# Seven-product quads in two value chunks and in one more run of both down projections

## The chip, the cores and the metric

The kernel runs on one NeuronCore of a Trainium2 chip. The metric is the device time of one execution in microseconds; before the change it is 2053.36 us, the median of three runs (2053.22 to 2055.54). Engines are named as the profile names them: PE is TensorE (PEld its weight loads), DVE is VectorE, ACT is ScalarE, POOL is GpSimd, SP is SyncE, which here only issues DMAs.

## The reference

Two decoder layers over 256 tokens of width 2048, in float32. Each layer is attention, a residual with LayerNorm, a gated feed-forward, and a residual with LayerNorm:

```python
q, k, v = split(x @ w_qkv)                   # layer 1: 16 heads of 128, causal, T5 bias
attn = softmax(q k^T * scale + bias) v @ w_o
h = layer_norm(ALPHA * h + attn)
hc = causal_conv3(h @ w_up) + conv_b         # 2 x 5504 features
g, u = split(hc)
h = layer_norm(ALPHA * h + (gelu(g) * u) @ w_down)
```

With 256 tokens and blocks of 256, layer 1's block-sparse attention is plain causal attention. Layer 2 takes a window of 128 tokens with learned sinks, and its 16 query heads share 4 key and value heads. The result must match in float32.

## The kernel before

**Precision.** TensorE multiplies in a rounded format, so every operand is kept as a high part and a low part: for weights ScalarE copies the raw tile to `wh` (L160) and VectorE subtracts to get `wl` (L169). A product takes three matmuls: high x high, high x low, low x high (L530 to L532; L385 to L387 in the value projections). The fourth is dropped.

**Halves.** Weights stream from HBM as *halves*, 128 x 1024 floats (512 KB), two blocks of 128 x 512. SP loads each into one of six `raw` tiles (L141); the split goes into one of four pairs `wh`, `wl`; TensorE takes them in order. The next load of a raw tile is issued once VectorE's split has read it. One half is one *slot* of the written schedule: `at(n, f)` puts f into the agenda n slots ahead, and `take` (L204) first asks for the splits up to three halves ahead and then runs the agenda. So each engine's order is fixed by the program, and an operation of the agenda stands between the splits on VectorE's queue.

**Two kinds of products.** Queries, keys and up projections hold the weights still (`ws_unit`, two halves, 32 matmuls). Values, output and down projections hold the tokens still and move the weights: a *plain* half has 2 blocks x 2 token tiles x 3 = 12 matmuls of 512 columns.

**Quads.** Where the plan of a projection says so (`PLAN_O`, `PLAN_DOWN`, made by `_mixed`), a 2 x 2 group of tokens and output chunks is done with seven products in place of eight (Strassen-Winograd). One *run* of quads covers four blocks of the contraction and a pair of 512-wide output chunks: seven halves of 6 matmuls (`SEVEN`) in place of four plain halves of 12. It needs

- combined weights, T1 to T4: *presums* (L426) load a quad's four blocks (two DMAs of 512 KB on SP), combine them with four VectorE operations (L436) and store them to HBM (two DMAs on POOL); they run during earlier projections, one quad every 6 or 8 slots, through one buffer `gb`;
- combined activations: `sums` (L582), three steps in successive slots: `whole` (L588), `combine` (three or four operations, L599) and `split` (ScalarE L604, VectorE L605). They are kept in `xT` and a further tile;
- the accumulators P1, P5, P6, P7 (PSUM banks named `at`), which `fold` adds into the result at the end of a chunk pair. The plain products and the rest go to four banks named `acc`, one for each (chunk, token tile).

`PLAINS` and `PLAINS_O` say how many plain halves stand before, between and after the runs. In a down projection (43 blocks, four chunks) each chunk pair has six runs; in the first pair 2 plain halves stand between most runs, in the second pair 1, and 15 at the end. The last eight halves of a projection are its *window*: first all of token tile 0, then all of token tile 1, so that LayerNorm of tile 0 runs under the matmuls of tile 1. An accumulator is emptied (`evac`: L547 or L549 adds it into the residual, L553 takes the LayerNorm statistics) after both token tiles of its chunk are complete; for odd chunks one and two slots later.

**Layer 1's attention** goes over four groups of four heads: a value chunk of 8 plain halves (`v_group`), then for each head a query unit and a key unit, with the softmax of the head before it spread over the next slots. Each bias table for the softmax is spread through HBM: a row table `ud`, four DMAs to `band` (L297; layer 1's on POOL, layer 2's on ACT), and four loads of `bias` (L301). The residual input comes in two DMAs of 1 MB on SP at slots 55 and 70.

Of the kernel before, what the change touches and what calls it, by code (L numbers as in the profile page):

```python
# [2 lines left out]

# [8 lines left out]
F32 = mybir.dt.float32  # L12
# [35 lines left out]
PLAINS = ((5, 2, 2, 2, 2, 0, 6), (0, 1, 1, 1, 1, 0, 15))  # L48
NQ_O = 4
PLAINS_O = (5, 3, 0)  # L50
SEVEN = (("B11", "B21"), ("T1", "T3"), ("T2", "T4"), ("B22", "B22"), ("B11", "B21"), ("T1", "T3"), ("T2", "T4"))
# [10 lines left out]
def _mixed(c, groups, plain, p0):  # L62

    plan, at = [], 0
    for i, g in enumerate(groups):
        plan += plain[at:at + g]
        at += g
        if i < len(groups) - 1:
            plan += [tuple((b, p0 + 2 * i + p, c) for b, p in zip(bs, ps)) for bs, ps in zip(SEVEN, PAIR_OF)]
    assert at == len(plain)  # L70
    return plan
# [3 lines left out]
PLAN_DOWN = [h for c in range(2) for h in _mixed(c, PLAINS[c], _plain(range(2 * NQ, FT), (2 * c, 2 * c + 1)), 0)]  # L75
QUADS = {}
for _l in range(2):
    QUADS[2 * _l] = [(2 * _l, 0, NH // 2 - NQ_O + p) for p in range(NQ_O)]
    QUADS[2 * _l + 1] = [(2 * _l + 1, c, p) for c in range(2) for p in range(NQ)]
ORDER = [q for li in range(4) for q in QUADS[li]]  # L80
AHEAD_OF = {0: QUADS[0] + QUADS[1][:8], 1: QUADS[1][8:] + QUADS[2], 2: QUADS[3][:4], 3: QUADS[3][4:]}
# [7 lines left out]
def _stages():  # L89

    for l in range(2):
        yield [None] * (48 if l else 96), 0
# [6 lines left out]
def trunk(ctx: ExitStack, tc: tile.TileContext, wst, wsum, xT_in, x_in, relb, onehot, umask, sinks, conv_in, ln_g, ln_b, out):  # L99
# [128 lines left out]

    def load_input(pool, tables):
# [65 lines left out]
    def spread_bias(l, h0, h1):  # L295
        a = ud[l, h0:h1, :]
        (nc.scalar if l else nc.gpsimd).dma_start(band[l, h0:h1], bass.AP(tensor=a.tensor, offset=a.offset + P - 1,  # L297
# [128 lines left out]
    def presums(quads, first_slot, pitch):  # L426
# [18 lines left out]
        for i, q in enumerate(quads):  # L445
            m = first_slot + pitch * i
            at(m, load, q, 0)
            at(m + 1, load, q, 1)
            for j, x in enumerate(steps):
                at(m + 4 + j, step_of, *x)  # L450
                if j % 2:
                    at(m + 4 + j, store, q, j // 2)

    def project_out(src, plan, li, homes, preload, turnover=None, quad_blocks=None):
# [41 lines left out]
        banks, used, owed = {}, {}, {}  # L496

        def token(x, t):
            return x[:, t * P:(t + 1) * P], x[:, T + t * P:T + (t + 1) * P]

        def keys(e):
            b, k, n = e
            if b == "plain":
                return [(n, t) for t in range(2)]
            n0, n1 = 2 * n, 2 * n + 1
            return [{"B11": ("P1", n), "B21": (n0, 0), "T1": ("P5", n), "T3": ("P7", n), "T2": ("P6", n), "T4": (n0, 1),
                     "B22": (n1, 0)}[b]]

        def target(e):
            b, k, n = e  # L510
            if b == "plain":
# [578 lines left out]
```

## Time and profile before

| | |
|---|---|
| runs, median (lowest to highest) | 2053.36 us (2053.22 to 2055.54) |
| the profiled execution, its own time | 2053.82 us |
| its span, first to last instruction | 2052.1 us |
| mean granted TensorE clock | 0.998 |
| mean DMA rate | 276 GB/s |
| first value chunk of the third group | 154.5 to 176.3 us |
| output projection, layer 1 | 298 to 388 us |
| up projection, layer 1 | 388 to 870 us |
| down projection, layer 1 | 870 to 1090 us |
| down projection, layer 2 | 1821 to 2040 us |

Of the profile, a group's row has its line, engine, operation, tiles, count, busy time, mean duration and idle time before it; a row of waits has what waited, for what, us in total, times, longest; a row of the order in time has start, duration, engine, line, operation, and in brackets the idle time before it with what ended it. A stretch has for each engine its busy time and instruction count, then the granted clock, the DMA engines' busy share and GB/s.

### The profile page before, as it was taken

To read this page: it belongs to the slowest core of one execution; us is meant where nothing else is said; L and a number is where in the kernel's file an instruction comes from. 1 tells how busy PE (TensorE), PEld (TensorE's weight loads), DVE (VectorE), ACT (ScalarE), POOL (GpSimd) and SP (SyncE) were. 2 spreads that over 40 slices of the span, in tenths; PEclk is the share of its full clock that TensorE was granted. 3 is DMA by queue.
4 is the path that set the end of the run, shared out by engine and by line. 5 is a ranking of instruction groups with operands and counts; after the bars stand their busy time and mean duration, and the time that the engine had idled before them with its cause. 6 is when DMAs were issued, how large, how long until landed. Compare 5 with 4: busy or idle time off the path is not lost.

```text
span 2052.1 us, 29718 instructions
## 1 busy us (share of the span) xinstructions
PE 2036.1 (99%) x10908; PEld 1759.3 (86%) x10908; DVE 1675.9 (82%) x2399; ACT 1138.3 (55%) x1676; POOL 75.4 (4%) x138
## 2 busy tenths in 40 slices
PE   9999999999999999999999999999999999999997
PEld 7888888988888888888888888898888888888886
DVE  5676678888888888899896788978888888889887
ACT  5444456455555555566673556545555555556672
POOL 0100000000000000000000000000000000000000
PEclk9999999999999999999999999999999999999999
DMA  8888988468888888888994767838888888889893
GB/s 297 287 281 328 320 287 313 162 238 282 289 288 273 282 296 269 285 286 329 323 366 156 261 217 252 285 126 275 281 286 283 279 283 291 272 266 328 312 361 150
DMA packets 158722, 566.64 MB, mean 276 GB/s; under 512 B 19008, under 2 KB 21376, under 8 KB 157296
## 3 DMA queue, kind: packets, MB, share of 16 engines
q1 hardware_dynamic: 136064, 492.74, 70.7%
q0 software_dynamic: 20160, 69.64, 8.7%
q10 hardware_dynamic: 2352, 2.36, 0.3%
q8 instruction: 86, 1.41, 0.3%
q14 instruction: 60, 0.49, 0.1%
HBM read 503.78 MB, written 65.06 MB: 277 GB/s over the span
## 4 chain that ended last, share of the span: by engine, by line
PE 98%; DVE 1%; DMA 0%; ACT 0%; issue 0%; ACTq 0%; DVEq 0%
PE acc L322 39%; PE acc L324 20%; PE acc L530 7%; PE acc L531 7%; PE acc L532 7%; PE at L532 2%; PE at L531 2%; PE at L530 2%; PE acc L386 2%; PE acc L385 2%; PE acc L387 2%; PE acc L349 1%; PE acc L361 1%; PE at L722 1%; PE at L755 1%; PE at L748 1%
## 5 line engine op out<-in xcount | busy, mean ns | idle before, releaser
L169 DVE TENSOR_TENSOR wl<-raw,wh 128x1024 fp32r<-128x1024 f32 (+1 forms) x754 | 898.8, 1220 | 186.4 <-ACT wh L160 163.9
L160 ACT ACTIVATE wh<-raw 128x1024 fp32r<-128x1024 f32 (+1 forms) x754 | 770.4, 1052 | 207.9 <-PE acc L532 104.5
L322 PE MATMUL acc<-xT,wh 128*128 128x512 f32 x3456 | 832.8, 392 | 0.0
L322 PEld LDWEIGHTS acc<-xT,wh 128*128 128x128 f32 x3456 | 641.1, 188 | 128.6
L324 PEld LDWEIGHTS acc<-xT,wl 128*128 128x128 f32 x3456 | 444.2, 190 | 12.4
L324 PE MATMUL acc<-xT,wl 128*128 128x256 f32 x3456 | 452.5, 284 | 0.0
L909 ACT ACTIVATE h<-acc 128x256 f32<-128x256 f32 x172 | 66.4, 386 | 409.1 <-PE acc L324 203.1
L917 DVE SCALAR_TENSOR_TENSOR c<-h,cw,c 128x255 f32<-128x255 f32 x344 | 165.4, 481 | 9.1 <-ACT c L913 2.8
L436 DVE TENSOR_TENSOR gb<-gb 128x512 f32<-128x512 f32 x224 | 153.5, 685 | 5.9 <-DMA gb<-in_wsum_dram 5.9
L910 DVE TENSOR_TENSOR h<-acc,h 128x256 f32<-128x256 f32 x172 | 72.7, 423 | 64.2 <-ACT h L909 64.2
L440 POOL DMA_DIRECT2D ws<-gb x112 | 59.8, 534 | 1412.1 <-DVE gb L436 1360.3
L530 PE MATMUL acc<-wh,up 128*128 128x512 f32 x275 | 107.0, 389 | 0.0
L531 PE MATMUL acc<-wl,up 128*128 128x512 f32 x275 | 107.0, 389 | 0.0
L532 PE MATMUL acc<-wh,up 128*128 128x512 f32 x275 | 107.0, 389 | 0.0
L913 ACT ACTIVATE c<-h,cw 128x256 f32<-128x256 f32 x172 | 101.7, 591 | 0.0
L530 PE MATMUL acc<-wh,st 128*128 128x512 f32 x174 | 68.8, 395 | 0.0
L531 PE MATMUL acc<-wl,st 128*128 128x512 f32 x174 | 67.8, 390 | 0.0
L532 PE MATMUL acc<-wh,st 128*128 128x512 f32 x174 | 67.8, 390 | 0.0
L831 ACT ACTIVATE qT<-acc 128x256 f32<-128x256 f32 x32 | 12.3, 385 | 91.3 <-PE acc L324 65.9
L532 PEld LDWEIGHTS acc<-wh,up 128*128 128x128 f32 x275 | 51.6, 188 | 10.7
L530 PEld LDWEIGHTS acc<-wh,up 128*128 128x128 f32 x275 | 51.6, 188 | 10.7
L531 PEld LDWEIGHTS acc<-wl,up 128*128 128x128 f32 x275 | 51.6, 188 | 10.6
(193 smaller groups left out, 2152.5 us busy)
## 6 DMA issues: line engine op xcount, KB each, us to landing
raw<-in_wst_dram SPq DMA_DIRECT2D x694, 512.0 KB, 5.2
gb<-in_wsum_dram SPq DMA_DIRECT2D x112, 512.0 KB, 7.6
ws<-gb POOLq DMA_DIRECT2D x112, 512.0 KB, 6.2
raw<-ws SPq DMA_DIRECT2D x112, 512.0 KB, 5.6
bias<-band POOLq DMA_DIRECT2D x8, 512.0 KB, 7.2
band<-ud POOLq DMA_DIRECT2D x4, 512.0 KB, 12.7
band<-ud ACTq DMA_DIRECT2D x4, 512.0 KB
res<-in_x_dram SPq DMA_DIRECT2D x2, 1024.0 KB, 9.4
```

Of the source, the lines that this page charges most:

```text
L160: nc.scalar.activation(wh[:, c], raws[s][:, c], AF.Copy)
L169: nc.vector.tensor_tensor(out=wl[:, c], in0=raws[s][:, c], in1=wh[:, c].bitcast(F32), op=ALU.subtract)
L322: nc.tensor.matmul(acc, w, xT[:, k, :], start=(k == 0), stop=(k == ends[0]))
L324: nc.tensor.matmul(acc[:, 0:T], w, xT[:, k, 0:T], start=False, stop=(k == ends[1]))
L436: nc.vector.tensor_tensor(out=w[:, o:o + 512], in0=a, in1=b, op=op)
L530: nc.tensor.matmul(acc, sh, wh, start=first, stop=False)
L531: nc.tensor.matmul(acc, sh, wl, start=False, stop=False)
L532: nc.tensor.matmul(acc, sl, wh, start=False, stop=last)
L909: nc.scalar.activation(h, acc[:, T:2 * T], AF.Copy)
L910: nc.vector.tensor_tensor(out=h, in0=acc[:, 0:T], in1=h, op=ALU.add)
L913: nc.scalar.activation(c, h, AF.Identity, bias=w[:, 3:4], scale=w[:, 2:3])
L917: nc.vector.scalar_tensor_tensor(c[:, d:T], h[:, 0:T - d], w[:, 2 - d:3 - d], c[:, d:T], op0=ALU.mult, op1=ALU.add)
```

## The change

In layer 1 the value chunks of the third and fourth group are computed together by `v_pair`, before the third group's heads: `PLAN_V` has 5 plain halves, a run, 3 plain halves, a run (22 halves in place of 16). Their accumulators are copied by ScalarE and added by VectorE into the value tiles.

In both down projections the second chunk pair gets a seventh run. All seven now follow each other without a plain half between them, in the order 4, 0, 1, 2, 3, 5, 6, and the 15 remaining plain halves follow. The sums of the seventh run have all four parts; they are computed eleven slots into the second pair and written over the sums of run 4 (`last_sums`), which is why run 4 goes first.

An accumulator is emptied as soon as it alone is complete, also inside the window (`late`): chunk 2 now ends in the window's first half. The code of quads is moved into a function `mixed` that both users call, without another change.

The presums have eight more quads (64 in place of 56). In layer 1's attention they start at slot 16 in place of 22, in the up projections they are spread evenly over 152 slots (one in about 7) in place of one in 8. Layer 1's bias spreading goes to slots 4, 6, 8, 10 (three of the four on ACT's queue), layer 2's from slots 40, 47, 76, 82 to 76, 82, 88, 94.

```diff
-PLAINS = ((5, 2, 2, 2, 2, 0, 6), (0, 1, 1, 1, 1, 0, 15))
+MORE = 2
+RUNS = (range(6), (4, 0, 1, 2, 3, 5, 6))
+PLAINS = ((5, 2, 2, 2, 2, 0, 6), (0, 0, 0, 0, 0, 0, 0, 15))
...
+PLAN_V = _mixed(1, PLAINS_O, _plain(range(KB - 2 * NQ_O), (2, 3)), KB // 2 - NQ_O)
-PLAN_DOWN = [h for c in range(2) for h in _mixed(c, PLAINS[c], _plain(range(2 * NQ, FT), (2 * c, 2 * c + 1)), 0)]
+PLAN_DOWN = [h for c in range(2) for h in _mixed(c, PLAINS[c], _plain(range(2 * (NQ + MORE * c), FT), (2 * c, 2 * c + 1)), 0, RUNS[c])]
...
-AHEAD_OF = {0: QUADS[0] + QUADS[1][:8], 1: QUADS[1][8:] + QUADS[2], 2: QUADS[3][:4], 3: QUADS[3][4:]}
+QUADS[4] = [(4, 1, KB // 2 - NQ_O + p) for p in range(NQ_O)]
+ORDER = [q for li in (4, 0, 1, 2, 3) for q in QUADS[li]]
+AHEAD_OF = {0: QUADS[4] + QUADS[0] + QUADS[1][:6], 1: QUADS[1][6:] + QUADS[2], 2: QUADS[3][:4], 3: QUADS[3][4:]}
...
+    def last_sums():
+        flat = xT[:, KB - 4:KB, :].rearrange("p a b -> p (a b)")
+        return flat.rearrange("p (h q s c) -> p h q s c", h=2, q=2, s=4)
...
-        (nc.scalar if l else nc.gpsimd).dma_start(band[l, h0:h1], bass.AP(tensor=a.tensor, offset=a.offset + P - 1,
+        (nc.scalar if l or h0 else nc.gpsimd).dma_start(band[l, h0:h1], bass.AP(tensor=a.tensor, offset=a.offset + P - 1,
...
         def late(t, i):
             last = i == WINDOW - 1
+            for n in range(NCH - 1):
+                if (n, t) not in evacuated and done((n, t)):
+                    evacuated.add((n, t))
+                    evac(n, t)
...
+            if ns == 3:
+                for j, f in enumerate(sums(NQ // 2)):
+                    at(whole + 11 + j, f)
...
             for n in range(NCH):
-                if n not in evacuated and done((n, 0), (n, 1)):
-                    evacuated.add(n)
-                    for t in range(2):
-                        at((t + 1) * (n % 2), evac, n, t)
+                for t in range(2):
+                    if (n, t) not in evacuated and done((n, t)):
+                        evacuated.add((n, t))
+                        at(t * (n % 2) * (ns == 3), evac, n, t)
...
-                at(4 + 5 * i, spread_bias, 0, h, h + 4)
-                at((40, 47, 76, 82)[i], spread_bias, 1, h, h + 4)
-            at((4 + 5 * i, 4 * i)[l], load_bias, bias, l, h, h + 4)
+                at(4 + 2 * i, spread_bias, 0, h, h + 4)
+                at((76, 82, 88, 94)[i], spread_bias, 1, h, h + 4)
+            at((5 + 2 * i, 4 * i)[l], load_bias, bias, l, h, h + 4)
...
+        def v_pair():
+            src = lambda k: xT[:, k, :]
+            k0 = KB - 2 * NQ_O
+            vts, begun = {}, set()
...
+            def into(t, n, a):
+                if n not in vts:
+                    vts[n] = pool.tile([P, 2, 512], F32, name="vt", bufs=2)
+                d = vts[n][:, t, :]
+                if (t, n) in begun:
+                    nc.vector.tensor_tensor(out=d, in0=d, in1=a, op=ALU.add)
+                else:
+                    begun.add((t, n))
+                    nc.scalar.activation(d, a, AF.Copy)
+
+            parted = mixed(src, PLAN_V, k0 // 2, lambda i: 4, lambda i: xT[:, k0 + 4 * i:k0 + 4 * i + 4, :], place, into)
+            mv = Moving(src, 0)
+            for i in range(len(PLAINS_O) - 1):
+                for j, f in enumerate(parted.sums(i)):
+                    at(sum(PLAINS_O[:i]) + 7 * i + j, f)
+            evacuated = set()
+            for half in PLAN_V:
+                blocks = [mv.block() for _ in range(2)]
+                for e, w in zip(half, blocks):
+                    for tgt in parted.target(e):
+                        parted.product(*tgt, *w)
+                step()
...
+            parted.fold(1)
...
-        presums(AHEAD_OF[2 * l], 3 if l else 22, 8 if l else 6)
+            presums(ahead, [16 + 6 * i for i in range(len(ahead))])
...
-            presums(AHEAD_OF[2 * l + 1], 4, 8)
+            presums(ahead, [4 + 152 * i // (len(ahead) - 1) for i in range(len(ahead))])
```

More of the change, by code (lines that the diff above doesn't have):

```diff
@@ L2 @@
 from contextlib import ExitStack
+from types import SimpleNamespace
 import numpy as np
@@ L59, in _plain, with _mixed @@
     return [tuple(blocks[i:i + 2]) for i in range(0, len(blocks), 2)]
-def _mixed(c, groups, plain, p0):
+def _mixed(c, groups, plain, p0, runs=None):
     plan, at = [], 0
@@ L68, in _mixed @@
         if i < len(groups) - 1:
-            plan += [tuple((b, p0 + 2 * i + p, c) for b, p in zip(bs, ps)) for bs, ps in zip(SEVEN, PAIR_OF)]
+            r = runs[i] if runs else i
+            plan += [tuple((b, p0 + 2 * r + p, c) for b, p in zip(bs, ps)) for bs, ps in zip(SEVEN, PAIR_OF)]
     assert at == len(plain)
@@ L424, in acc_tile, with presums @@
         return psum.tile([P, 512], F32, name="acc")
-    def presums(quads, first_slot, pitch):
+    def presums(quads, slots):
         area = gbp.tile([P, 2, D], F32, name="gb")
@@ L444, in presums @@
                  (1536, b21, w[:, 1024:1536], ALU.subtract))
-        for i, q in enumerate(quads):
-            m = first_slot + pitch * i
+        for m, q in zip(slots, quads, strict=False):
             at(m, load, q, 0)
@@ L494, in project_out @@
         ag, rs = {}, {}
[L496 to L511, printed above, removed]
[L512 to L535 removed]
         def zs(t, n):
             return res[:, t, n * 512:(n + 1) * 512]
+        parted = mixed(src, plan, p0, lambda i: ns + (2 * i >= NQ), quad_blocks, lambda i: xsum(i, ns) if 2 * i < NQ else last_sums(), lambda t, n, a: into(t, n, a))
+        banks, target, product, done, fold, sums = (parted.banks, parted.target, parted.product, parted.done, parted.fold,
+                                                    parted.sums)
         paired = {e[2] for half in plan for e in half if e[0] == "B11"}
@@ L823, in v_group, with place @@
             return vt
+        def v_pair():
+            src = lambda k: xT[:, k, :]
+            k0 = KB - 2 * NQ_O
+            vts, begun = {}, set()
+            def place(i):
+                flat = st[:, NH // 2 + 4 * i:NH // 2 + 4 * i + 4, :].rearrange("p a b -> p (a b)")
+                return flat.rearrange("p (h q s c) -> p h q s c", h=2, q=2, s=4)
+            def into(t, n, a):
[4 more added lines that the diff above has]
+                    nc.vector.tensor_tensor(out=d, in0=d, in1=a, op=ALU.add)
+                else:
+                    begun.add((t, n))
[12 more added lines that the diff above has]
+                step()
+                for n in (2, 3):
+                    for t in range(2):
+                        if (n, t) not in evacuated and parted.done((n, t)):
+                            evacuated.add((n, t))
+                            at(0, lambda n=n, t=t: into(t, n, parted.banks.pop((n, t))))
+            parted.fold(1)
+            run(before)
+            return vts
         def feat_unit(name, bufs):
```

168 lines of the change are left out of this document (100 added, 68 removed).

## The prediction

> **What bounds the kernel now.** I read the page's busy times and the chain of waits first, then the waits of TensorE, and last the order in time of each engine around the places that change.
>
> ```profile
> span 2052.1 us, 29718 instructions
> PE 2036.1 (99%) x10908; PEld 1759.3 (86%) x10908; DVE 1675.9 (82%) x2399; ACT 1138.3 (55%) x1676; POOL 75.4 (4%) x138
> PE 98%; DVE 1%; DMA 0%; ACT 0%; issue 0%; ACTq 0%; DVEq 0%
> PE acc L530 <- DVE res L549: 1.0, 2, 0.5
> PE acc L530 <- DVE res L547: 0.8, 2, 0.4
> 306.61 0.39 PE L530 MATMUL acc<-wh,st 128*128 128x512 f32 x1
> ...
> 309.33 0.39 PE L530 MATMUL acc<-wh,st 128*128 128x512 f32 x1
> ```
>
> TensorE sets the end: 98% of the chain is its matmuls, and it waits almost only at four places, twice in each kind of projection, for VectorE to empty an accumulator (1.0 + 0.8 us). The two timeline rows are twelve matmuls apart, one plain half: 2.72 us, so **0.227 us a matmul** (the 0.39 us are overlapping durations). A quad half has six matmuls: 1.36 us.
>
> What the change can lose shows in the second chunk pair of the first down projection, where quads already stand almost without plain halves between them: ScalarE's and VectorE's order in time, and three stretches.
>
> ```profile
> 997.57 1.06 ACT L160 ACTIVATE wh<-raw 128x1024 fp32r<-128x1024 f32 x1 [0.30 <-PE acc L532]
> 998.93 1.06 ACT L160 ACTIVATE wh<-raw 128x1024 fp32r<-128x1024 f32 x1 [0.30 <-PE acc L532]
> 982.84 0.68 DVE L547 TENSOR_TENSOR res<-res,acc 128x512 f32<-128x512 f32 x1
> 983.56 0.69 DVE L553 BATCH_NORM_STATS2 stats<-res 128x6 f32<-128x512 f32 x1
> 984.17 1.21 DVE L169 TENSOR_TENSOR wl<-raw,wh 128x1024 fp32r<-128x1024 f32 x1
> 985.29 0.68 DVE L547 TENSOR_TENSOR res<-res,acc 128x512 f32<-128x512 f32 x1
> 986.01 0.69 DVE L553 BATCH_NORM_STATS2 stats<-res 128x6 f32<-128x512 f32 x1
> 986.62 5.75 DVE L169 TENSOR_TENSOR wl<-raw,wh 128x1024 fp32r<-128x1024 f32 x5
> 993.22 2.59 DVE L169 TENSOR_TENSOR wl<-raw,wh 128x1024 fp32r<-128x1024 f32 x2 [0.85 <-ACT wh L160]
> 1026.00:1048.00 22.00, 22.00 (x99) 18.22 (x98) 19.10 (x16) 16.72 (x17) 0.00 (x0) 1.00 0.99 377
> 1955.00:1977.00 22.00, 22.00 (x99) 18.22 (x98) 19.13 (x16) 16.55 (x16) 0.00 (x0) 1.00 0.96 350
> 388.00:870.00 482.00, 482.00 (x2834) 428.21 (x2833) 398.85 (x616) 263.65 (x430) 20.92 (x40) 1.00 0.79 268
> ```
>
> ScalarE starts a half every 1.36 us, each time when TensorE gives a buffer back: the split runs as far ahead as four buffers let it. That lead is small. TensorE gives back the pair of half h-4 and wants h three halves (4.08 us) later; between lie ScalarE's 1.06, VectorE's 1.21 and about 0.1 for each hand-over, so **about 1.7 us** are left. Five splits in a row take 5.75, that is (5.75 - 1.21)/4 = 1.13 us each: in a run of quads VectorE wins back only 1.36 - 1.13 = **0.23 us a half**, where a plain half gives 1.36 more. The last two numbers of a stretch are the DMA share and GB/s: at 0.96 to 0.99 the DMA engines are nearly full too.
>
> **The change part by part.**
>
> *TensorE.* A run of quads is 7 x 6 = 42 matmuls in place of 48. Two runs in the value pair and one in each down projection remove 24: 24 x 0.227 = **-5.45 us**. Nothing hides TensorE's work, so all of it is on the path.
>
> *Accumulators one by one.* In the output projections the accumulators (1,1) and (1,0) are now emptied well before chunk 2 asks for banks; I give the whole wait back, -1.0. In the down projections each emptying moves one slot forward, past one split, and the wait of 0.8 goes; but VectorE works without a gap from 982.84 to 992.37, the two emptyings (1.33 us each with their statistics) now stand before the splits of halves 65 and 66, and the second of these comes late by some 0.4. I keep -0.2 of the 0.8 (ends 0 and -0.8). Sum **-1.2 us**.
>
> *The dense pair of each down projection.* The plain halves at 68, 76, 84 and 92 go to the end; 49 quad halves follow each other. Eleven slots into the pair stand the sums for the seventh run, in VectorE's order among the splits. Their durations are those of the output projection's:
>
> ```profile
> 326.44 1.22 DVE L588 TENSOR_TENSOR tmp<-st 128x1024 f32<-128x1024 f32 x1
> 329.16 1.68 DVE L599 TENSOR_TENSOR tmp<-tmp 128x256 f32<-128x256 f32 x4
> 331.97 1.23 DVE L605 TENSOR_TENSOR xT<-tmp,xT 128x1024 fp32r<-128x1024 f32 x1
> ```
>
> Less the overlap of about 0.09 each, that is 1.13 + 1.59 + 1.13 = 3.85 us, and three splits between them 3.4: 7.25 us against 4.08 of TensorE and the lead of 1.7. TensorE waits **1.5 us**, twice, +3.0 (ends: 1.0 if the emptyings' delay has gone by then and hand-overs cost nothing, 2.5 if it has not: seven halves win back 1.6). What is queued behind them is the splits of halves 76 to 78, and TensorE waits for exactly these. There the trace before had plain halves as cover; it has none left.
>
> Each dense half also needs 512 KB in 1.36 us, 385 GB/s, against 377 at a share of 0.99. At 377 a half takes 1.39: 49 x 0.03 = 1.5 us, which the six loaded raw tiles (8.2 us) cover. What they do not cover is a single late load, as in the second down projection:
>
> ```profile
> 1944.69 1.06 ACT L160 ACTIVATE wh<-raw 128x1024 fp32r<-128x1024 f32 x1 [0.30 <-PE acc L532]
> 1947.91 1.06 ACT L160 ACTIVATE wh<-raw 128x1024 fp32r<-128x1024 f32 x1 [2.16 <-DMA raw<-ws]
> ```
>
> This one came 1.86 us later than the pace and a lead of 1.7 took it. After the sums the lead is zero for some eight halves of 49. Ends 0 and 1.9 in each layer; I take 0.5, since most would meet a full lead: **+1.0**.
>
> *The value pair* takes 8 x 2.72 + 14 x 1.36 = 40.8 us of TensorE in place of 43.5 (the gain is counted above). The presums of later projections go on in it, one quad in six slots, and the residual's first MB is loaded in the eighth slot. VectorE has 22 splits (24.9), two sets of sums (7.7), 14 presum operations (L436 below, 9.6) and the last head's softmax (about 3): 45 us against 40.8 and a lead that is 3 x 2.72 - 2.4 = 5.8 us at plain pace: covered, or late by a few tenths at the end of the second run, where the lead has shrunk to 1.7. More can come from the loads that the presums wait for, because VectorE takes its work in order:
>
> ```profile
> L436 DVE TENSOR_TENSOR gb<-gb 128x512 f32<-128x512 f32 x224 | 153.5, 685 | 5.9 <-DMA gb<-in_wsum_dram 5.9
> 170.13 0.42 SPq L433 DMA_DIRECT2D gb<-in_wsum_dram  x1
> 171.08 0.43 SPq L433 DMA_DIRECT2D gb<-in_wsum_dram  x1
> 177.83 0.69 DVE L436 TENSOR_TENSOR gb<-gb 128x512 f32<-128x512 f32 x1 [1.90 <-DMA gb<-in_wsum_dram]
> 181.07 0.69 DVE L436 TENSOR_TENSOR gb<-gb 128x512 f32<-128x512 f32 x1 [1.41 <-DMA gb<-in_wsum_dram]
> ```
>
> Here the loads took 7.7 and 10.0 us; four quad slots are 5.4. But they shared the DMA engines with the spreading of the bias table of layer 2, which the change moves out of this stretch. Ends 0 and 4; I take **+0.7**, near the lower.
>
> *Bias tables.* Three quarters of layer 1's table go through ScalarE's queue at slots 6, 8 and 10, all but at once with the first on GpSimd's.
>
> ```profile
> 28.22 1.12 POOL L297 DMA_DIRECT2D band<-ud  x1 [4.44 <-DMA ud<-us]
> 41.51 0.79 POOL L301 DMA_DIRECT2D bias<-band  x1 [12.17 <-DMA band<-ud]
> 46.69 0.29 DVE L726 SCALAR_TENSOR_TENSOR L<-at,bias 128x128 f32<-128x128 f32 x1 [1.95 <-DMA bias<-band]
> ```
>
> VectorE already waits 1.95 us for the first bias, TensorE not yet. The three tables beside it can make it later, and the splits behind it too. Ends 0 and 3 (a quarter more on the 13.3 us to 41.51); I take **+0.4**.
>
> *Costed at nothing.* The eight more quads bring 32 presum operations, 16 loads and 16 stores. In layer 1's up projection they add 4 x 4 x 0.69 = 11 us to VectorE's 399 of 482 (stretch above), the DMA engines are far from full there at 268 GB/s, and the splits there are waited for by nobody; without that cover they would cost up to those 11 us. SP's loads of raw halves stand behind the presum loads and those behind VectorE, as before. In the last window chunk 2 now ends one half inside: one emptying with statistics (1.37 us) moves between the first token tile's norms and its low parts, which have this idle time before the last emptying:
>
> ```profile
> 1088.04 0.69 DVE L639 TENSOR_TENSOR xT<-at,xT 128x512 fp32r<-128x512 f32 x1 [0.84 <-ACT xT L634]
> 1089.87 0.69 DVE L639 TENSOR_TENSOR xT<-at,xT 128x512 fp32r<-128x512 f32 x1 [1.14 <-ACT xT L634]
> ```
>
> 1.98 us take 1.37; without them the end of the layer would move by 1.37.
>
> **The sum:** -5.45 - 1.2 + 3.0 + 1.0 + 0.7 + 0.4 = -1.55 us. The profiled execution took 2053.82 us (its span 2052.1 and 1.7 around it), 0.46 above the median of the three runs and inside them: 2053.8 - 1.5 = **2052.3 us**.
>
> **The rivals.**
>
> *A: nothing new waits.* VectorE has more lead than I count, or the sums fit between splits. For it: in the output projection the same sums, at the times shown, cost TensorE nothing. Against it: there three plain halves cover them. Then -5.45 - 1.8 and perhaps one remaining wait of 0.5 to 1 in each layer: about **2048**, at best 2053.8 - 7.25 = 2046.6.
>
> *B: the DMA engines cannot feed quads without plain halves (slower).* Its place is the value pair and both dense pairs. In the value pair each of three quads' presums waits as at 177.83 and 181.07 (3.3 us each, 9.9), less a lead of 1.7 and three plain halves' 4.1: +4. In each dense pair two loads as late as that at 1947.91 meet no lead: 3.7, twice. Sum: -5.45 - 1.2 + 3.0 + 7.4 + 4 + 0.4 = +8.2, **2062 us**. It decides once new waits come to more than 5.45 + 1.2 = 6.7 us in all. For it: 350 GB/s at a share of 0.96, where 385 are wanted. Against it: 377 in the stretch beside it, with TensorE's matmuls unbroken.
> The Trainium skill, DMA: Bandwidth & Descriptors, section Bandwidth, says that between HBM and SBUF a core's share of HBM, some 358 GB/s, is what binds, though a core whose neighbour is idle was measured higher. By the 358 a dense half takes 1.46 us and each dense pair falls 49 x 0.10 = 5 us behind, and this rival would be the likeliest. The trace's 377 over 22 us disagrees with that limit here, so its chance stays small.
>
> *C: the accumulators still wait*, because banks are handed out in another order than I read. For it: four such waits exist. Against it: in the output projections the two that chunk 2 gets are now emptied three and seven halves ahead. Then +1.2 on the forecast, 2053.5 us.
>
> **How the numbers follow.** Chances: forecast 0.50, C 0.11, A 0.25, B 0.14. What a measurement of this kernel can tell from no change is about 0.2%, 4.1 us: below 2049.7 is faster, above 2057.9 slower (of 2053.8). Forecast and C lie within, save for their tails, 0.02 each way. A counts as faster, B as slower: faster 0.27, same 0.57, slower 0.16. The forecast's own range, from its bounds, is 2050 to 2056; for 8 in 10 it reaches to most of A and the near part of B: 2047.6 to 2057.6.
>
> **What would show it.** *TensorE:* 24 matmuls fewer, and half spacing 1.36 us in the runs. *Accumulators:* the waits for the residual gone from TensorE's list. *Dense pair:* a wait of TensorE for VectorE's splits of about 1.5 us, some twelve to sixteen halves into the second chunk pair, in both layers; without it A is right. *Loads:* ScalarE's waits for raw in the dense pairs below 1 us each; several of 2 us, and TensorE waiting behind them, mean B. *Value pair:* its 22 halves in 41 to 42 us. *Bias:* the first softmax of layer 1 delayed by less than 3 us, TensorE unbroken. The forecast is wrong if the new waits sum to less than 1 us or to more than 9.

## The result, and the profile after

The changed kernel takes **2072.35 us** (median of 4; 2071.87 to 2074.60), the kernel before 2054.08 on the same chip: a ratio of 1.0091, 95% interval 1.0076 to 1.0106. I had forecast 2052.3, with 2057.6 as the upper end: wrong by 20 us and in sign.

The page of the changed kernel (span, busy times, the chain's shares by engine, the presum operations), and then its list of TensorE's waits (us in total, times, longest). L179 is VectorE's split of a weight half, L170 ScalarE's, L557 and L558 the high and low part of a run's sums, L450 a presum operation.

```profile
span 2070.5 us, 29932 instructions
PE 2039.1 (98%) x10884; PEld 1756.8 (85%) x10884; DVE 1722.6 (83%) x2475; ACT 1154.9 (56%) x1693; POOL 80.8 (4%) x151
PE 83%; DMA 6%; issue 5%; DVE 4%; ACT 1%; ACTq 1%; POOL 0%; SPq 0%; DVEq 0%; POOLq 0%
L450 DVE TENSOR_TENSOR gb<-gb 128x512 f32<-128x512 f32 x256 | 175.3, 685 | 15.4 <-DMA gb<-in_wsum_dram 15.2
```

```profile
PE acc L338 <- DVE wl L179: 6.4, 2, 4.6
PE at L505 <- DVE wl L179: 4.2, 7, 1.1
PE at L506 <- DVE st L558: 3.8, 1, 3.8
PE acc L505 <- DVE wl L179: 1.4, 2, 0.7
...
PE at L504 <- ACT st L557: 1.3, 1, 1.3
```

TensorE has its 24 matmuls fewer (10908 to 10884) and the waits for the residual are gone: the change does what it says. But the chain is TensorE's for 83% instead of 98%, and five new rows of waits come to 17 us, where 9 was my own limit. Where the time went can be read off the first matmul of each stage in TensorE's order in time (us; the last stage ends at the start of the last matmul; the work removed is 12 and 6 matmuls of 0.227). In the kernel before, the third value chunk's first matmul is at 151.80, not at 154.5 as the table of the profile before has it:

| stretch | before | after | difference | of it work removed |
|---|---|---|---|---|
| start to the second value chunk | 78.55 | 85.88 | +7.33 | 0 |
| third value chunk to the first output projection | 146.51 | 153.65 | +7.14 | -2.72 |
| output projections | 89.62, 90.61 | 88.80, 89.83 | -0.82, -0.78 | 0 |
| first up projection | 482.05 | 482.05 | 0 | 0 |
| down projections | 220.39, 218.56 | 222.89, 222.11 | +2.50, +3.55 | -1.36 each |

These sum to +18.9; the end behind the last matmul is 0.5 shorter, and the spans differ by 18.4. So three things have to be explained: 7.3 us at the start, 7.14 + 2.72 = 9.9 in the value pair, and 3.9 and 4.9 in the down projections. I read each in the changed kernel's order in time.

*The start*, ScalarE (start, duration, engine, line; in brackets the idle time before and what ended it; ACTq are the instructions that issue DMAs, L311 the spreading of a bias table):

```profile
27.78 1.18 ACTq L311 DMA_DIRECT2D band<-ud  x1
29.08 1.06 ACT L170 ACTIVATE wh<-raw 128x1024 fp32r<-128x1024 f32 x1 [3.45 <-issue]
29.11 8.85 ACTq L311 DMA_DIRECT2D band<-ud  x1
38.00 0.60 ACT L848 ACTIVATE vt<-acc 128x512 f32<-128x512 f32 x1 [7.86 <-issue]
38.16 8.58 ACTq L311 DMA_DIRECT2D band<-ud  x1
...
46.84 2.01 ACT L170 ACTIVATE wh<-raw 128x1024 fp32r<-128x1024 f32 x2 [6.54 <-issue]
```

ScalarE computes nothing for 7.9 and 6.5 us, because its own queue stands at the issue of the second and third table. Splits behind them are late, VectorE's after them, and TensorE waits. Its row of 6.4 us holds two waits; by stretches of time only the first is here, the second stands behind the value pair (window 20 to 60, then 160 to 226):

```profile
PE acc L338 <- DVE wl L179: 4.6, 1, 4.6
```

```profile
PE acc L338 <- DVE wl L179: 1.8, 1, 1.8
```

After the wait the granted clock is half for some 5 us (0.50, shown in the last section), so that the same matmuls take some 2.5 us longer (an estimate from the clock); 4.6 and 2.5 are nearly the 7.3.

*The value pair*, VectorE, then TensorE at the same place:

```profile
185.75 0.69 DVE L450 TENSOR_TENSOR gb<-gb 128x512 f32<-128x512 f32 x1 [1.82 <-DMA gb<-in_wsum_dram]
...
198.69 0.69 DVE L450 TENSOR_TENSOR gb<-gb 128x512 f32<-128x512 f32 x1 [2.62 <-DMA gb<-in_wsum_dram]
199.30 1.22 DVE L558 TENSOR_TENSOR st<-tmp,st 128x1024 fp32r<-128x1024 f32 x1
```

```profile
200.57 0.80 PE L506 MATMUL at<-wh,st 128*128 128x512 f32 x1 [3.79 <-DVE st L558]
201.16 0.63 PE L504 MATMUL at<-wh,st 128*128 128x512 f32 x1
...
203.30 0.45 PE L506 MATMUL at<-wh,st 128*128 128x512 f32 x1
```

A presum waits for its load, the second run's sums wait behind it in VectorE's order, and TensorE waits 3.8 us for them. The 1.3 for ScalarE (L557) is just ahead of it, the 1.8 behind the pair. The matmuls after the wait are 0.43 us apart ((203.30 - 201.16)/5), not 0.227; of that below.

*A dense pair* (first down projection), VectorE, then TensorE:

```profile
1011.83 1.22 DVE L541 TENSOR_TENSOR tmp<-up 128x1024 f32<-128x1024 f32 x1
1012.96 1.22 DVE L179 TENSOR_TENSOR wl<-raw,wh 128x1024 fp32r<-128x1024 f32 x1
1014.10 1.67 DVE L552 TENSOR_TENSOR tmp<-tmp 128x256 f32<-128x256 f32 x4
1015.69 1.22 DVE L179 TENSOR_TENSOR wl<-raw,wh 128x1024 fp32r<-128x1024 f32 x1
1016.89 1.22 DVE L558 TENSOR_TENSOR xT<-tmp,xT 128x1024 fp32r<-128x1024 f32 x1
```

```profile
1016.96 0.50 PE L505 MATMUL at<-wl,xT 128*128 128x512 f32 x1 [1.06 <-DVE wl L179]
...
1019.30 0.50 PE L505 MATMUL acc<-wl,xT 128*128 128x512 f32 x1 [0.69 <-DVE wl L179]
```

The sums of the seventh run alternate with splits as predicted, and TensorE waits for exactly those splits. (By the starts of its matmuls a wait costs some 0.3 us more than the list has: a matmul that the list lets wait 0.3 starts 0.67 after the one before it, not 0.227.)

### The profile page after: what moved, and what is told of

Its sections match the earlier page's. It is cut to its first block, busy times and chain, and to the rows that moved or that the text cites. A ratio compares the mean times of both kernels' runs of the same rounds, so it can differ in the third digit from the quotient of the medians.

```text
span 2070.5 us, 29932 instructions
## 1 busy us (share of the span) xinstructions
PE 2039.1 (98%) x10884; PEld 1756.8 (85%) x10884; DVE 1722.6 (83%) x2475; ACT 1154.9 (56%) x1693; POOL 80.8 (4%) x151
## 4 chain that ended last, share of the span: by engine, by line
PE 83%; DMA 6%; issue 5%; DVE 4%; ACT 1%; ACTq 1%; POOL 0%; SPq 0%; DVEq 0%; POOLq 0%
PE acc L336 36%; PE acc L338 19%; PE acc L506 6%; PE acc L504 6%; PE acc L505 6%; DMA raw<-in_wst_dram 3%; DVE wl L179 2%; PE at L505 2%; PE at L506 2%; PE at L504 2%; PE acc L363 1%; DMA raw<-ws 1%; DMA gb<-in_wsum_dram 1%; ACT wh L170 1%; PE acc L375 1%
## 5 line engine op out<-in xcount | busy, mean ns | idle before, releaser
L179 DVE TENSOR_TENSOR wl<-raw,wh 128x1024 fp32r<-128x1024 f32 (+1 forms) x766 | 911.8, 1219 | 169.2 <-ACT wh L170 153.1
L170 ACT ACTIVATE wh<-raw 128x1024 fp32r<-128x1024 f32 (+1 forms) x766 | 782.5, 1052 | 204.7 <-PE acc L506 89.3
L450 DVE TENSOR_TENSOR gb<-gb 128x512 f32<-128x512 f32 x256 | 175.3, 685 | 15.4 <-DMA gb<-in_wsum_dram 15.2
L454 POOL DMA_DIRECT2D ws<-gb x128 | 68.5, 535 | 1430.0 <-DVE gb L450 1368.4
L505 PE MATMUL acc<-wl,up 128*128 128x512 f32 x251 | 97.7, 389 | 0.0
L504 PE MATMUL acc<-wh,up 128*128 128x512 f32 x251 | 97.7, 389 | 0.0
L506 PE MATMUL acc<-wh,up 128*128 128x512 f32 x251 | 97.7, 389 | 0.0
L899 ACT ACTIVATE qT<-acc 128x256 f32<-128x256 f32 x32 | 12.3, 385 | 84.0 <-PE acc L338 58.6
L504 PEld LDWEIGHTS acc<-wh,up 128*128 128x128 f32 x251 | 47.1, 188 | 9.8
L506 PEld LDWEIGHTS acc<-wh,up 128*128 128x128 f32 x251 | 47.1, 188 | 9.8
L505 PEld LDWEIGHTS acc<-wl,up 128*128 128x128 f32 x251 | 47.1, 188 | 9.7
```

The lines of the kernel that those rows point to most:

```text
L170: nc.scalar.activation(wh[:, c], raws[s][:, c], AF.Copy)
L179: nc.vector.tensor_tensor(out=wl[:, c], in0=raws[s][:, c], in1=wh[:, c].bitcast(F32), op=ALU.subtract)
L450: nc.vector.tensor_tensor(out=w[:, o:o + 512], in0=a, in1=b, op=op)
L454: nc.gpsimd.dma_start(wsums[q][:, js], w[:, js])
L504: nc.tensor.matmul(acc, sh, wh, start=first, stop=False)
L505: nc.tensor.matmul(acc, sh, wl, start=False, stop=False)
```

## The experiments

Stage times below are worked out as in the table, from each run's own trace. They differ from execution to execution by one to three us. Three of the kernels below are the changed kernel up to the first down projection (the sums left out, and plain halves back, twice): there the first stretch takes 86.8 to 88.2 and the value pair's 154.5 to 155.5. Five others leave the down projections as the change has them: there these take 222.6 to 226.0 and 220.2 to 221.5.

### One part undone or taken out

**Tables on GpSimd's queue again.**

```diff
-        (nc.scalar if l or h0 else nc.gpsimd).dma_start(band[l, h0:h1], ...
+        (nc.scalar if l else nc.gpsimd).dma_start(band[l, h0:h1], ...
```

> The changed kernel with one line undone: all of layer 1's bias tables go through GpSimd's queue again, at the changed slots. Theory: ScalarE issues two of the tables itself and its own queue is held for 8.85 and 8.58 us meanwhile; the splits behind it, VectorE's after them and TensorE's matmuls wait. Without that the stretch to the end of the second value chunk goes from 85.9 back to about 78.6 us, TensorE's wait of 6.4 us for VectorE's splits is gone, and the kernel takes about 2065. Rival: four tables spread within 13 us crowd the DMA engines whichever queue issues them; then the wait stays but for 2 us, and the time is 2070 or more.

2074.61 us (1.0098, 1.0083 to 1.0113): no gain. Yet the first stretch fell to 78.83, as the theory has it; the next one lost it again (82.09 in place of 73.25). GpSimd's and VectorE's order in time (L315 loads a bias table, L454 stores presums):

```profile
86.87 0.78 POOL L315 DMA_DIRECT2D bias<-band  x1 [14.96 <-DMA band<-ud]
87.65 1.10 POOL L454 DMA_DIRECT2D ws<-gb  x2
```

```profile
96.07 0.69 DVE L450 TENSOR_TENSOR gb<-gb 128x512 f32<-128x512 f32 x1 [7.79 <-DMA ws<-gb]
```

The last table's load waits for its spreading until 86.87, the first presum stores stand behind it, a presum operation waits for the store, and the softmax behind that: TensorE waits 5.8 us at 97. The change had moved the first presum from slot 22 to 16, and that is what the tables' new queue made room for: in the changed kernel the last table's load goes out at 68.11 and the first store at 78.82. The theory on ScalarE is not refuted, but a single undo could not price it.

**Tables on ScalarE's queue, but further apart.**

```diff
-                at(4 + 2 * i, spread_bias, 0, h, h + 4)
+                at(4 + 5 * i, spread_bias, 0, h, h + 4)
-            at((5 + 2 * i, 4 * i)[l], load_bias, bias, l, h, h + 4)
+            at((5 + 5 * i, 4 * i)[l], load_bias, bias, l, h, h + 4)
```

> The changed kernel with the same queues for layer 1's bias tables (three on ScalarE's), but one every five slots instead of every two. With all four on GpSimd's queue the wait at 41 us went, and another of 6.0 us came at 97, since presum stores stood behind the last table there. Theory: an issue holds ScalarE's queue for as long as the table before it is still being written (1.18 us for the first, 8.85 and 8.58 for the next two); 12 to 15 us apart each costs about 1.2, TensorE's 6.4 us of waits go, and the stretch to the end of the second value chunk is 79 us again: 2065. Rival: the length of an issue comes from its 512 rows of 1 KB, whatever is under way; then two or three waits of 4 to 8 us stay, 2070 or more.

The group of the issues on ScalarE's queue (shortest, median, longest in ns), of this kernel and of the changed one:

```profile
L311 ACTq DMA_DIRECT2D band<-ud x7: 597/613/1177, 30.1 to 282.8; - x7
```

```profile
L311 ACTq DMA_DIRECT2D band<-ud x7: 597/614/8848, 27.8 to 287.0; - x7
```

The same seven issues of the same tables: none above 1.2 us when they are apart, 8.85 when two stand behind one another. The first stretch takes 78.72 us. So the theory holds, and the number of rows does not set the length. The kernel's time was 2068.61 (2064.89 to 2071.42), less of a gain than 7.2; the profiled execution was the slowest, with 52.7 us in the value pair and 225.99 in the first down projection. The spread comes up again below.

**No presums in the value pair.**

```diff
-AHEAD_OF = {0: QUADS[4] + QUADS[0] + QUADS[1][:6], 1: QUADS[1][6:] + QUADS[2], ...
+AHEAD_OF = {0: QUADS[4] + QUADS[0] + QUADS[1][:2], 1: QUADS[1][2:] + QUADS[2], ...
-            presums(ahead, [16 + 6 * i for i in range(len(ahead))])
+            presums(ahead, [m for m in range(16, 95, 6) if not 46 <= m <= 64])
```

> The changed kernel without presums in the value pair: the four quads of slots 46, 52, 58 and 64 are summed in layer 1's up projection instead. Theory: the pair needs 17.7 MB in 51 us (347 GB/s at a DMA share of 0.95), more than the DMA engines bring in the 40.8 us that TensorE needs; 3.7 quads of 2 MB less leave some 11 MB, the pair takes 41 to 42 us in place of 50.6, and the kernel 2063 to 2064. Rival: the splits alone, at four buffers, cannot keep up with two runs of quads (hand-overs, sums, the second value chunk's fold); then the pair stays above 46 us and the kernel above 2068.

2102.63 us. The pair took 43.4 us, but 28 quads in the up projection stand five or six slots apart; at five a load overwrites `gb` before the last operation has read it, so these sums are not those of the weights, and the up projection took 521.5 us in place of 482.05. Four quads of the second layer moved to that layer mend it:

```diff
+AHEAD_OF = {0: QUADS[4] + QUADS[0] + QUADS[1][:2], 1: QUADS[1][2:], 2: QUADS[2], 3: QUADS[3]}
```

> The changed kernel without presums in the value pair, and no two quads of presums less than six slots apart: ten in layer 1's attention, 24 in its up projection, four in layer 2's attention, 26 in its up projection. (With 28 in the first up projection, five or six slots apart, a load overwrote a buffer before its last reading, the sums were not those of the weights, and that stage lost 39 us; but its value pair took 43.4 us, and from there to the output projection 143.7 in place of 153.6.) Theory (bytes and order in the value pair): those 9.9 us stay won and both up projections stay at 457: 2062 to 2063. Rival: the presums cost as much where they go; 2068 or more.

2062.11 us (1.0041, 1.0026 to 1.0057): 10.2 less than the changed kernel, as expected. (The 457 is an up projection without its opening; it stayed.) The value pair as a stretch (length, then busy us and instructions of PE, PEld, DVE, ACT and POOL, the granted clock, the DMA share, GB/s), changed kernel first:

```profile
159.10:209.70 50.60, 45.55 (x198) 36.76 (x197) 43.11 (x56) 28.84 (x36) 3.60 (x7) 0.97 0.95 348
```

```profile
159.10:202.50 43.40, 43.40 (x198) 36.04 (x197) 36.71 (x44) 28.73 (x36) 0.42 (x1) 1.00 0.81 284
```

50.6 us at 348 GB/s are 17.6 MB. In the 43.4 us that TensorE needs here (40.8 for the 22 halves, the rest for the last head's matmuls), that is 406 GB/s. The highest that any of these traces has over 43.4 us is 408. Without presums it is 12.3 MB. The residual's first MB, still loaded there, costs nothing that can be seen: from the pair to the output projection it takes 143.70 us, and 146.51 - 2.72 is 143.79.

**The loads alone taken out.** The kernel leaves out the loads of the four quads; operations and stores stay, so these sums are not those of the weights.

```diff
+            if slots[0] != 16 or not 46 <= m <= 64:
                 at(m, load, q, 0)
                 at(m + 1, load, q, 1)
```

> The changed kernel with the loads of those four quads left out: VectorE's operations and the stores stay, on what the buffer holds from before, so four quads' sums are not those of the weights. It tells a wait for the loads from VectorE's work. If the wait for the loads and the bytes decide: 7 to 8.5 us less, the pair at 42 to 44 us, the kernel near 2064.5. If VectorE's sixteen added operations (11 us) decide: the pair falls by less than 2 us, the kernel stays at 2070 or more.

2065.00 us (1.0053, 1.0038 to 1.0068). The stretch to the output projection takes 147.10, 6.55 less. So of the 9.95 us that the presums cost here (153.65 less 143.70), two thirds is the loads: their bytes and the wait for them, which this run does not separate. The rest goes with the stores and VectorE's sixteen operations, which it leaves in; a wait of 1.3 for the second run's sums is left.

**The seventh run's sums left out.**

```diff
-            if ns == 3:
-                for j, f in enumerate(sums(NQ // 2)):
-                    at(whole + 11 + j, f)
```

> The changed kernel with the seventh run's sums left out in both down projections, so that its products use what the buffer holds. It prices the prediction's term for the sums alone: by the prediction each pair loses 1.5 us less and keeps 0.5 of late loads. If the waits of 1.2, 0.9 and later ones go, the down projections take 218 to 219 in place of 222.9 and 222.1, and the sums cost more than the 3.85 us of their own beyond the lead. If they stay above 221, the density of quads costs it.

2066.64 us, one execution; its products use what the buffer holds. The down projections take 218.95 and 218.28: 3.94 and 3.83 less than in the changed kernel's profile. Against the five kernels with the same down projections it is 3.7 or more in the first layer and 1.9 to 3.2 in the second. What is left is 0.45 us (by the starts) at the half behind the accumulators' emptyings in each layer and one late load in the second; ScalarE there:

```profile
1962.53 1.06 ACT L170 ACTIVATE wh<-raw 128x1024 fp32r<-128x1024 f32 x1 [1.01 <-DMA raw<-ws]
...
1966.53 1.06 ACT L170 ACTIVATE wh<-raw 128x1024 fp32r<-128x1024 f32 x1 [1.71 <-DMA raw<-in_wst_dram]
```

TensorE loses 1.0 us to it (0.8 in the list). So forty-nine quad halves on end cost about half a us in the first layer and one and a half in the second, and the sums 2 to 4.

**The accumulators one by one, in the kernel before.**

```diff
+                for t in range(2):
+                    if (n, t) not in evacuated and done((n, t)):
+                        evacuated.add((n, t))
+                        at(t * (n % 2) * (ns == 3), evac, n, t)
```

> The kernel before with one part of the change: each accumulator is emptied when its own sums are done, not both together. By the prediction the output projections lose their waits (1.0 in all) and the down projections 0.2: 1.2 us less, all waits for the residual gone from TensorE's list but for some 0.3 each in the down projections. If banks are handed out in another order (rival C), nothing changes: both waits stay.

2053.68 us (0.9995, 0.9986 to 1.0005): not to be told from no change. TensorE's list:

```profile
PE at L632 <- DVE res L623: 0.8, 1, 0.8
PE at L531 <- DVE wl L169: 0.6, 2, 0.3
```

The waits for the residual's accumulators are gone, so rival C falls; 0.3 in each down projection takes their place, and 0.8 in the first output projection's last window. By stages only the second output projection wins (89.86, before 90.61).

### The three stalls mended

**Plain halves back between the runs.**

```diff
-PLAINS = (..., (0, 0, 0, 0, 0, 0, 0, 15))
+PLAINS = (..., (0, 2, 1, 1, 1, 0, 0, 10))
-                    at(whole + 11 + j, f)
+                    at(whole + 7 + j, f)
```

> The changed kernel with five plain halves put back between the seven runs of the second chunk pair in both down projections (2, 1, 1, 1, and ten at the end), and the sums of the seventh run in the slots of the first two of them. Nothing is added or taken from TensorE. Theory: the plain halves give VectorE its lead back; TensorE's waits of 5.0 and 6.0 us in the two pairs fall to below 1 each, and the kernel takes 2063 to 2064. Rival: only the 3.8 us of sums matter or late loads come whatever the order; then the two layers win 2 us each at most, 2068 or more.

2077.93 us. With ten plain halves at the end, the first layer's last window splits a half onto sums that the last run has yet to read, which changes its result and holds TensorE for 8.9 us. The second layer, without such a window, took 216.85 us, 5.3 less. So eleven:

```diff
+PLAINS = (..., (0, 2, 1, 1, 0, 0, 0, 11))
```

> The changed kernel with four plain halves back between the seven runs of the second chunk pair (2, 1, 1, and eleven at the end), and the seventh run's sums in the slots of the first two. (With ten at the end the window's first splits landed on sums that the last run still had to read, in layer 1, which cost 9 us and was not the sum wanted; its layer 2, which has no such window, took 216.85 us in place of 222.1.) Theory: TensorE's waits in both pairs shrink to half a us, each down projection takes about 217.3, and the kernel 2062 to 2063. Rival, that late loads come whatever the order: 2068 or more.

2073.64 us (1.0093, 1.0079 to 1.0107). The second layer takes 217.09, as expected; the first 225.05, which is more than the changed kernel's. TensorE's list:

```profile
PE at L653 <- DVE res L644: 4.4, 1, 4.4
```

The four waits of the dense pair have become one in the last window, where the transposes wait for the norms.

**All three edits together.** The tables five slots apart, the presums moved, four plain halves back.

> The three edits in one: tables five slots apart, no presums in the value pair, plain halves back between the runs. If the three stalls are separate, their gains add: 7.2 + 9.9 + 10 off 2072.3, about 2045, below the kernel before. If one uncovers another (later presums against the second up projection, tables against the first presums), 2050 or more.

2058.99 us (2053.42 to 2061.83; 1.0018, 1.0009 to 1.0026): neither theory. The first two gains are whole in the trace; the first down projection's window keeps a wait of 4.3. ScalarE ahead of that window:

```profile
1065.54 1.06 ACT L170 ACTIVATE st<-raw 128x1024 fp32r<-128x1024 f32 x1 [3.52 <-DMA raw<-in_wst_dram]
```

The window wants halves split far ahead, and their loads come late: as I read it, the plain halves at the end were what gave the loads and VectorE time for it.

**All fifteen at the end, the sums spread out.**

```diff
-                for j, f in enumerate(sums(NQ // 2)):
-                    at(whole + 11 + j, f)
...
+                total, combine, split = sums(NQ // 2)
+                at(whole + 16, total)
+                for j in range(4):
+                    at(whole + 21 + 3 * j, combine, j)
+                at(whole + 38, split)
```

> Tables five slots apart and no presums in the value pair, as in the run with the three edits; but all fifteen plain halves stay at the end of the second chunk pair, and the seventh run's six operations on VectorE (1.13, four of 0.40, 1.13 us) are spread over slots 16 to 38 of the pair in place of slots 11 to 13. In the run with three edits one wait of TensorE was left, 4.3 us in layer 1's last window: with eleven plain halves there, loads and VectorE came late. Theory: it is the sums' bunching that used up the lead, and the fifteen halves at the end are needed; each down projection takes 217 to 218.5, the kernel about 2046. Rival: forty-nine quad halves without a break are more than VectorE or the loads can follow, whatever the bunching; then the pairs still lose 3 us or more each, and the time is 2051 or more.

2058.37 us (1.0009, 0.9998 to 1.0021). The down projections take 221.49 and 220.09, with nine waits of at most 0.5 each: 1.4 and 2.0 us less than in the changed kernel. Between the theories; and a wait of 1.4 for the softmax had come at 92 us.

**Two plain halves moved, thirteen kept.** As with all three edits, and `(0, 2, 0, 0, 0, 0, 0, 13)`.

> As in the run with the three edits, but only two plain halves are moved up, behind the first run of the pair and under the seventh run's sums (2, and thirteen at the end). Theory: two are enough for the sums, thirteen nearly enough for the last window: the pairs lose less than 1 us each, the window's wait falls from 4.3 to below 2, and the kernel takes 2046 to 2048. If thirteen are as short as eleven, the window's wait stays near 4 and the time near 2052 in the profile.

2055.08 us (2048.46 to 2058.06; 0.9999, 0.9990 to 1.0008). The profiled execution, at 2048.46 the fastest, has one wait of 1.2 in the window and the second down projection at 216.85. But most executions were 3 to 10 us slower.

**The same kernel, profiled a second time.**

> The kernel with tables five slots apart, no presums in the value pair and two plain halves moved up, profiled a second time. The first profile was its fastest execution (2048.5); most take 2051 to 2058. If presum stores behind the bias tables are the cause, this profile has a wait of TensorE near 92 us that the first has not, of 2 to 6 us; if the last window of the first down projection, its wait there is 3 us or more in place of 1.2.

2056.69 us. GpSimd, VectorE, TensorE's list, and the stretch behind the wait:

```profile
84.08 0.76 POOL L315 DMA_DIRECT2D bias<-band  x1 [19.87 <-DMA band<-ud]
84.83 1.10 POOL L454 DMA_DIRECT2D ws<-gb  x2
```

```profile
95.38 0.69 DVE L450 TENSOR_TENSOR gb<-gb 128x512 f32<-128x512 f32 x1 [7.56 <-DMA ws<-gb]
```

```profile
PE at L776 <- DVE L L771: 5.6, 1, 5.6
```

```profile
97.00:101.00 4.00, 4.00 (x11) 3.23 (x11) 3.20 (x4) 0.49 (x1) 0.53 (x1) 0.50 0.60 192
```

The wait seen with the tables on GpSimd's queue: the last table's load came 20 us after the one before it, the presum stores behind it, and TensorE waited 5.6 us. Value chunk two took 32.4 us where the first profile has 24.6: 7.9 of the 8.2 us between the two. In the first profile the load came 14.5 us after the one before it, and no such wait followed.

**The first presum at slot 22 again**, as in the kernel before:

```diff
+AHEAD_OF = {0: QUADS[4] + QUADS[0] + QUADS[1][:1], 1: QUADS[1][1:], 2: QUADS[2], 3: QUADS[3]}
+            presums(ahead, [m for m in range(22, 95, 6) if not 46 <= m <= 64])
```

> The same with the first presum at slot 22, as in the kernel before, in place of 16 (nine quads in layer 1's attention, 25 in its up projection). Presum stores then stand behind no bias table. If these are the cause of the slower executions, the executions draw together to 2047 to 2051 and the median is about 2049; if not, the median stays at 2054 to 2056 with the same spread.

**2048.45 us** (2046.35 to 2049.39), a ratio to the kernel before of **0.9965, 0.9953 to 0.9978**. The executions draw together. (One quad went from layer 1's attention to its up projection with it.) Its page and TensorE's list:

```profile
span 2044.9 us, 29958 instructions
PE 2030.7 (99%) x10884; PEld 1755.6 (86%) x10884; DVE 1723.3 (84%) x2475; ACT 1155.2 (56%) x1693; POOL 80.5 (4%) x151
...
PE 96%; DVE 2%; DMA 1%; ACT 0%; issue 0%; ACTq 0%; DVEq 0%
```

```profile
PE at L281 <- POOL ident masks.py:199: 1.4, 1, 1.4
PE at L505 <- DVE wl L179: 0.6, 2, 0.3
PE acc L400 <- DVE wl L179: 0.5, 1, 0.5
PE at L506 <- DVE st L558: 0.4, 1, 0.4
```

The same 10884 matmuls and 2475 operations of VectorE as in the changed kernel, in another order: 24 us less.

**One plain half moved, fourteen kept, the sums spread out**, else as the last: `(0, 1, 0, 0, 0, 0, 0, 14)`.

> As the one before, but one plain half behind the first run of the pair, fourteen at the end, and the seventh run's sums spread over slots 16 to 38. If the last window of the first down projection is what varies, this draws the executions together (2047 to 2050) where the other does not; if late loads between the runs are, it is slower by 2 to 4 us than the other.

2047.94 us (0.9963, 0.9950 to 0.9977): the same as the other within the intervals. Both beat both kernels.

## Why the prediction was wrong, point by point

**TensorE -5.45: right.** 24 matmuls fewer, and the span of the mended kernel (first presum at slot 22) lies 7.2 below that before.

**Accumulators -1.2: the mechanism right, the size not shown.** In the changed kernel the output projections won 0.82 and 0.78 (I gave 1.0 for both). Alone, in the kernel before, the waits went as well and the down projections kept 0.3 each, as argued; but the first output projection waited 0.8 in its window instead, and the interval of the time, -2.9 to +1.0 us, holds -1.2 as well as nothing.

**Dense pairs, sums +1.5 each: the mechanism right, the term too small.** It measured 3.94 and 3.83 from one profile to one profile, and 1.9 at the least. The step that failed is the subtraction of a full lead of 1.7 us: the emptyings had used it up, which the 0.45 us of waiting just ahead shows, and I kept that case as an end of 2.5. At the sums themselves the first layer loses 2.7. Nor did I count what comes later: TensorE meets the next delays with no lead, and in the two pairs it waits nine times where I had two waits.

**Late loads +1.0 for both: right in size, by one execution.** Without the sums one wait of 1.0 was left, in the second layer alone. The trace also bears on the bandwidth limit of the Trainium skill, DMA: Bandwidth & Descriptors, section Bandwidth. By some 358 GB/s, an estimate from that page, each pair would have fallen 5 us behind in its loads; about one us of waiting for loads showed in one pair. (I called this rival the likeliest by that figure; by my own count the loaded raw tiles, 8.2 us, would have covered those 5.) The mended kernel has in its first dense pair and just behind it

```profile
1000.00:1030.00 30.00, 30.00 (x134) 24.86 (x133) 27.10 (x23) 23.47 (x23) 0.00 (x0) 1.00 1.00 382
1017.00:1067.00 50.00, 50.00 (x222) 41.42 (x221) 47.13 (x44) 39.12 (x38) 0.00 (x0) 1.00 1.02 406
```

382 and 406 GB/s with TensorE unbroken, so the limit did not bind here. Nor is a DMA share of 1.00 by itself a stall: TensorE did not wait in either stretch.

**Value pair +0.7: the failed step.** It measured +9.9. The step is the price of the presums' loads: I added up VectorE's time and TensorE's, took the loads one at a time, and left out the sum of bytes, though I had done it for the dense pairs on the same page. The kernel before over a stretch as long, a plain value chunk and the query and key halves behind it:

```profile
151.80:195.30 43.50, 43.50 (x229) 37.33 (x228) 27.48 (x42) 19.26 (x32) 2.51 (x5) 1.00 0.90 344
```

That is 344 GB/s at a share of 0.90, or 15.0 MB; the pair has 17.6, 406 GB/s. What the runs show is that the pair takes 43.4 us unbroken without presums, and that two thirds of the loss hang on their loads. That it is the bytes, and not the order in which VectorE meets the loads, is argued: the pair would need as much as the traces show anywhere, but 406 GB/s was reached elsewhere without a wait. The end of 4 us that I kept was built on two late loads, one at a time, and not on a queue of them that stays behind. And some 3.4 us stay with the loads out, so my sum for VectorE (45 us, covered by a lead of 5.8) or the stores, counted at nothing, had a share too; which of them is open. My argument that the bias tables had left this stretch was true and too small: a table is 0.5 MB, the pair 17.6.

**Bias tables +0.4: the failed step, by its mechanism.** It measured +7.3 (8.3 to 9.7 in three other executions). I looked for a late table; the first arrived as before (GpSimd's load at 41.47, before at 41.51). I costed the issue of a DMA at nothing on the queue that issues it. The trace before had only issues far apart and could not show the hold, but a wait of 3.8 us of ScalarE's split for a table stood in its waits, and I did not follow it up.

**Moving the first presum from slot 22 to 16: not in the sum at all.** In the changed kernel it cost nothing, since the last table's load was out 10.7 us before the first store. With the tables five slots apart that load goes out at 78 to 84, with the stores right behind it, and moving the first presum back to slot 22 was worth some 6 us in the median.

**Costed at nothing: right.** The up projection with its presums took the same 482.05 us, and the last window, with fifteen halves, did not wait above 0.2 us.

**Rivals.** A and C fell. B had the direction, and its price for the value pair was nearer than mine; but the dense pairs lost to VectorE's sums and not to loads, so B is not what happened as a whole. No rival had the start.

## What to carry to other kernels

Before work is packed tighter, add up the bytes of the stretch, everything that is loaded there, over the new, shorter time, and hold it against the highest rate that a trace of the same kernel shows. Moving a DMA to another engine's queue changes two queues: what stands behind it on the new one, and what it had held up or made room for on the old one. A lead is spent once: where two bursts follow each other, subtract it from the first and refill it only at the rate that the row shows.

## What the runs showed of the hardware

**Issuing a DMA can hold the engine.** A table's spreading takes ScalarE's queue 0.6 to 1.2 us when the one before it was issued 13 us earlier or more, and 8.85 and 8.58 us when it was issued 1.3 and 9.1 us earlier; ScalarE computes nothing meanwhile. That it is the earlier transfer that holds the queue is inferred from the two spacings and from the 11 to 14 us that a table on GpSimd's queue takes to land; no run looked inside. The Trainium skill, DMA: Bandwidth & Descriptors, section Issuing engines are not separate DMA queues, calls the time to initiate a DMA usually small beside the DMA. Here, back to back, it was not: 8.85 us beside the 13 that a table takes to land.

**A long wait costs more than itself.** After TensorE's wait of 4.6 us at the start:

```profile
42.00:46.00 4.00, 4.00 (x14) 3.42 (x14) 0.00 (x0) 0.00 (x0) 1.03 (x2) 0.50 0.96 305
```

The granted clock is 0.50. After the wait of 5.6 us it was 0.50 over the next 4 us, with 11 matmuls where 17.6 fit; after 3.8 us six matmuls came at 0.43 us. After the waits of 1.06 and 0.69 in the dense pair the clock stayed at 1.00. The Trainium skill, TensorE: Matmul & The Clock Gate, section on the HAM clock gate, says that an idle window of about 3.4 us halves the clock until the array has been busy as long. These waits lie on both sides of it and agree. None of my terms counted this; by the granted clock the waits of 4.6, 3.8 and 5.6 cost some 2.5, 1.4 and 2.2 us more (estimates), and adding that to a wait of this length would have been nearer.
